# Both score maps of a token block in one three-bank PSUM tile, and a second bank for transposed probabilities

## The chip, the cores and the metric

The kernel runs on one core of one Trainium2 chip. The metric is the device time of one execution in microseconds (us). The engines are named as the profile names them: PE (TensorE, matmuls), DVE (VectorE), ACT (ScalarE), POOL (GpSimd) and SP (SyncE, which here issues the DMAs). PE writes its results to PSUM, which has eight banks of 2 KB in each partition (512 fp32 columns); DVE and ACT read them there.

## The reference

Two layers of a diffusion trunk. Each has a token-mixing part (a convolution branch and a differential-attention branch, merged by gates) and an MLP. There are 512 latent tokens and 256 context tokens; latent queries see all 768 keys, context queries the 256 context keys. In the second layer only the latent tokens have queries. What the change touches is the attention of one head:

```python
def block(qi):
    s = jnp.einsum('bqhcd,bkhcd->bhcqk', qi, keys,
                   preferred_element_type=jnp.float32) * scale
    p = jax.nn.softmax(s, axis=-1)
    w = p[:, :, 0] - lam * p[:, :, 1]
    return jnp.einsum('bhqk,bkhv->bqhv', w.astype(vals.dtype), vals)
```

Each of the 8 heads has two score maps (c = 0, 1), each with a softmax of its own; the weights are their difference.

## The kernel before, in words

Nearly all the work is matmuls in which fp32 operands are split into a high and a low part, so that one product takes three passes (`mm3`, lines 148 to 150: `qk` is the projection of queries and keys of the next head, `v` that of the values, both 256 columns a pass).

Attention runs head by head (`attend`, from line 960). A head has token blocks of 128 queries: four latent ones (t = 0 to 3, 768 keys) and, in the first layer, two context ones (t = 4, 5, 256 keys). For each block, `scores(t)` does for each of the two maps m: two passes over the keys on PE into a PSUM tile `S` (lines 988 and 990, in pieces of at most 512 columns), the row maximum on DVE (line 992), the exponential on ACT (line 995), which also sums the row. DVE then makes the weights of the difference in place (lines 999, 1000 and 1005: `e`). `turn(t)` transposes the weights on PE, three 128-key tiles at a time, into a PSUM tile `wT` (line 1018); ACT copies it into the high part `wth` and DVE subtracts for the low part `wtl` (lines 76 and 80, `split`). `values(u)` multiplies two blocks' transposed weights with the values into a PSUM tile `av`; `finish(u)` reduces its squares (`osq`, line 1044).

PSUM during attention: two banks for projections (pool `psA`), and what the pools `pS` and `pX` take. `pS` has two buffers for `S`; a map of 768 fp32 columns fills one and a half banks, and its tile takes two. `pX` has one bank with tag `tp` for `wT` and one with tag `av`. That is all eight.

The source runs a head's `scores`, `turn`, `values` and `finish` merged with filling work (projections of the next head, `qk` and `v`; for the last head the convolution's projections), by costs written in the yields. A scheduler then orders all instructions for each engine by a timing model of its own and the buffers that are free, and each engine works through its list in that order. A PSUM tile's buffer is given on when all that reads it is done. Between instructions of different engines on the same bank the framework puts a wait.

Of the kernel before, what the change touches and what calls it, by code (L numbers as in the profile page):

```python
# [8 lines left out]
F32 = mybir.dt.float32  # L9
# [5 lines left out]
P = 128  # L15
# [36 lines left out]
def trunk_kernel(  # L52
# [22 lines left out]
    def split(hi, lo, src, lo_eng=None):  # L75
        nc.scalar.activation(out=hi, in_=src, func=AF.Copy)  # L76
        with ExitStack() as later:
            if state["lows"]:
                later.enter_context(tc.issue_after(state["lows"]))
            return (lo_eng or nc.vector).tensor_tensor(out=lo, in0=src, in1=f32(hi), op=ALU.subtract)  # L80
# [65 lines left out]
    def mm3(ps, st, mv, first, last):  # L146
        (sh, sl), (mh, ml) = st, mv
        nc.tensor.matmul(ps, sh, mh, start=first, stop=False)  # L148
        nc.tensor.matmul(ps, sh, ml, start=False, stop=False)  # L149
        nc.tensor.matmul(ps, sl, mh, start=False, stop=last)  # L150
# [540 lines left out]
    for i in range(DEPTH):  # L691
# [13 lines left out]
        ap = apool.__enter__()  # L705
        state["tp"], state["nraw"] = ap, 1
        def tp_tile(name):
            return pX.tile([P, 512], F32, tag="tp", name=name)

        def hst(k, t):  # L710
            s = slice(t * P, t * P + P)
# [247 lines left out]
        def attend(h):  # L959

            QH, QL = QKt[h]
            vh, vl = Vt[h]
            U = {}

            def scores(t):
                u, j = t // 2, t % 2
                lat = u < 2
                nk, kb = (NTT, 0) if lat else (2, 4)
                nkey = nk * P
                if j == 0:  # L970
                    ng = 2 if lat else 1
                    U[u] = dict(
                        nk=nk, kb=kb, gw=nk // ng,
                        wT=[[ap.tile([P, 3, 256], F32R, tag=tg, name=f"{tg}{i}_{h}_{u}_{g}",
                                     bufs=3) for tg in ("wth", "wtl")] for g in range(ng)],
                        es2=ap.tile([P, 2], F32, tag="es2", name=f"es2{i}_{h}_{u}"))
                nm = f"{i}_{h}_{t}"
                ts = slice(t * P, t * P + P)
                es = []
                st = ap.tile([P, 8], F32, tag="st", name=f"st{nm}", bufs=4)  # L980
                for m in range(2):
                    S = pS.tile([P, 768], F32, tag="S", name=f"S{nm}_{m}")
                    for lo, hi in ((0, 512), (512, 768)):
                        lo = max(lo, kb * P)
                        if hi <= lo:
                            continue
                        o = slice(lo - kb * P, hi - kb * P)
                        nc.tensor.matmul(S[:, o], QH[:, m, ts], QH[:, 2 + m, lo:hi],
                                         start=True, stop=False)
                        nc.tensor.matmul(S[:, o], QL[:, m, ts], QH[:, 2 + m, lo:hi],  # L990
                                         start=False, stop=True)
                    nc.vector.tensor_reduce(out=st[:, m : m + 1], in_=S[:, :nkey], axis=AX.X,  # L992
                                            op=ALU.max, negate=True)
                    e = ap.tile([P, 768], F32, tag=f"e{m}", name=f"e{m}{nm}", bufs=2 - m)
                    nc.scalar.activation(out=e[:, :nkey], in_=S[:, :nkey], func=AF.Exp,  # L995
                                         bias=st[:, m : m + 1],
                                         accum_out=st[:, 2 + m : 3 + m])
                    es.append(e)
                nc.vector.reciprocal(st[:, 4:5], st[:, 3:4])
                nc.vector.tensor_scalar(st[:, 5:6], st[:, 4:5], st[:, 2:3], L["nlam"],  # L1000
                                        ALU.mult, ALU.mult)
                nc.gpsimd.tensor_tensor(out=st[:, 6:7], in0=st[:, 2:3], in1=st[:, 2:3],
                                        op=ALU.mult)
                nc.gpsimd.tensor_scalar(U[u]["es2"][:, j : j + 1], st[:, 6:7], EPS, None, ALU.mult)
                nc.vector.scalar_tensor_tensor(
                    out=es[0][:, :nkey], in0=es[1][:, :nkey], scalar=st[:, 5:6],
                    in1=es[0][:, :nkey], op0=ALU.mult, op1=ALU.add)
                W[t] = es[0]

            def turn(t):  # L1010
                u, j = t // 2, t % 2
                wt, gw = W.pop(t), U[u]["gw"]
                js = slice(j * P, j * P + P)
                for g, (th, tl) in enumerate(U[u]["wT"]):
                    tp = tp_tile(f"wT{i}_{h}_{t}_{g}")
                    for q in range(gw):
                        kk = g * gw + q
                        nc.tensor.transpose(tp[:, q * P : q * P + P],
                                            wt[:, kk * P : kk * P + P], ident)
                    split(th[:, :gw, js], tl[:, :gw, js],  # L1020
                          tp[:, : gw * P].rearrange("p (q d) -> p q d", q=gw))

            def values(u):
                d = U[u]
                nk, kb, gw = d["nk"], d["kb"], d["gw"]
                av = pX.tile([P, 512], F32, tag="av", name=f"av{i}_{h}_{u}")
                for kk in range(nk):
                    th, tl = d["wT"][kk // gw]
                    q = kk % gw
                    mm3(av[:, :256], (vh[:, kb + kk, :], vl[:, kb + kk, :]),  # L1030
                        (th[:, q, :], tl[:, q, :]), kk == 0, kk == nk - 1)
                sq = ap.tile([P, 256], F32, tag="osq", name=f"osq{i}_{h}_{u}", bufs=1)
                nc.scalar.activation(out=sq, in_=av[:, :256], func=AF.Square)
                uo = ap.tile([P, 256], F32, tag="uo", name=f"uo{i}_{h}_{u}")
                ended[:] = [nc.scalar.activation(out=uo, in_=av[:, :256], func=AF.Copy,
                                                 scale=L["ag"]).ins]
                nc.sync.dma_start(at_d[i][h, :, 256 * u : 256 * u + 256], uo)
                d["sq"], d["av"] = sq, av

            def finish(u):  # L1040
                d = U.pop(u)
                pc = d["av"][:, 256:258]
                for j in range(2):
                    nc.tensor.matmul(pc[:, j : j + 1], d["sq"][:, j * P : j * P + P],
                                     ones[:, 0:1], start=True, stop=True)
                r = rsall[:, h * qt_n + 2 * u : h * qt_n + 2 * u + 2]
                for j in range(2):
                    nc.scalar.activation(out=r[:, j : j + 1], in_=pc[:, j : j + 1],
                                         func=AF.Identity, scale=1.0 / P,
                                         bias=d["es2"][:, j : j + 1])  # L1050
                nc.gpsimd.tensor_tensor(out=r, in0=r, in1=mhalf[:, :2], op=ALU.pow)

            alone = h == H - 1
            W = {}
            nt = qt_n
            todo = []
            for t in range(nt):
                scores(t)
                yield 2.7 if t < 4 else 3.0 if alone else 0.9
                todo.append((0.7 if t < 4 else 0.25, turn, t))  # L1060
                if t % 2:
                    todo += [((2.0 if t < 4 else 0.7) + 2.0 * alone, values, t // 2),
                             (0.45 + 1.0 * alone, finish, t // 2)]
                if t == 0:
                    continue
                for _ in range(2):
                    if len(todo) > 1:
                        c_, f_, a_ = todo.pop(0)
                        f_(a_)
                        yield c_  # L1070
            carry.extend(todo)
# [88 lines left out]
        pS = pspool.__enter__()  # L1160
        psx = tc.tile_pool(name=f"psX{i}", bufs=1, space=PSUM, reuse_waits="tile")
        pX = psx.__enter__()
# [269 lines left out]
        for s in range(2):  # L1432
# [7 lines left out]
            for m in range(4):  # L1440
# [9 lines left out]
                for g in groups:  # L1450
                    rr[g.start] = gp.tile([P, 512], F32, tag="ar", bufs=3,
                                          name=f"mr{i}_{mb}_{g.start}")[:, : g.stop - g.start]
# [662 lines left out]
```

## Time and profile before

| | |
|---|---|
| median of 3 runs | 2258.76 us (2257.69 to 2258.91) |
| profiled execution, its own time | 2262.12 us |
| its span, first to last instruction | 2260.3 us |
| PE busy | 2217.1 us |
| DVE, ACT, POOL busy | 1651.7, 1045.5, 629.6 us |
| mean granted TensorE clock | 0.998 |

The profiled execution took 3.4 us more than the median; 1.8 us of its time lie outside the span. A matmul's record lasts longer than the distance to the next one, since they are pipelined, so a short pause of PE can hide in its busy time.

### The profile page before, as it was taken

What the parts mean: (1) busy time and instruction counts of PE and PEld (TensorE: products, weight loads), DVE (VectorE), ACT (ScalarE), POOL (GpSimd) and SP (SyncE); (2) the same over time, 40 slices, a digit from 0 to 9 for tenths busy, and PEclk for the clock granted to TensorE, in tenths of its full rate; (3) what the DMA queues carried; (4) which work ended last, traced back from release to release, by engine and by line L of the source; (5) the groups of instructions that cost most, each with busy time, mean ns of one, the idle gap of its engine ahead of it and who ended that gap; (6) DMA issues with size and microseconds to landing.
All of it is one profiled execution on the core that took longest, in us unless ns stands there. A gap on an engine that the chain in (4) does not pass through costs nothing.

```text
span 2260.3 us, 35793 instructions
## 1 busy us (share of the span) xinstructions
PE 2217.1 (98%) x14114; PEld 1999.1 (88%) x14114; DVE 1651.7 (73%) x2739; ACT 1045.5 (46%) x2035; POOL 629.6 (28%) x773
## 2 busy tenths in 40 slices
PE   8999999999999999999999999999999999999999
PEld 6999999888888999999999898999977888888887
DVE  6777777499767778788777457777769966657673
ACT  5555656432233264333445345565543333654541
POOL 1866666140000021111111346555613400000000
PEclk9999999999999999999999999999999999999999
DMA  9111101125354612332344521102114323443151
GB/s 310 57 48 45 48 29 49 64 98 171 128 176 140 205 50 64 108 115 91 131 145 144 173 76 57 46 27 64 45 61 162 117 82 127 144 143 100 56 186 38
DMA packets 202264, 232.59 MB, mean 103 GB/s; under 512 B 8864, under 2 KB 162928, under 8 KB 201968
## 3 DMA queue, kind: packets, MB, share of 16 engines
q1 hardware_dynamic: 202096, 230.30, 31.6%
q8 instruction: 111, 1.82, 0.3%
q14 instruction: 57, 0.47, 0.1%
HBM read 212.93 MB, written 17.35 MB: 102 GB/s over the span
## 4 chain that ended last, share of the span: by engine, by line
PE 77%; DVE 10%; POOL 4%; DMA 3%; ACT 3%; issue 2%; SPq 0%; DVEq 0%; POOLq 0%; ACTq 0%
PE r L157 4%; PE f L149 4%; PE f L150 3%; PE f L148 3%; PE r L148 3%; PE r L150 3%; PE r L149 3%; PE gt L148 3%; PE gt L149 3%; PE gt L150 3%; PE qk L148 2%; DMA ar<-in_w_ada_dram 2%; PE qk L149 2%; PE qk L150 2%; PE r L160 2%
## 5 line engine op out<-in xcount | busy, mean ns | idle before, releaser
L148 PE MATMUL qk<-h_wqk,h1h 128*128 128x256 f32 x640 | 183.7, 289 | 0.8 <-ACT h1h L76 0.7
L149 PE MATMUL qk<-l_wqk,h1h 128*128 128x256 f32 x640 | 181.1, 285 | 0.0
L150 PE MATMUL qk<-h_wqk,h1l 128*128 128x256 f32 x640 | 177.5, 285 | 0.0
L992 DVE TENSOR_REDUCE st<-S 128x1 f32<-128x768 f32 (+1 forms) x160 | 134.6, 846 | 52.2 <-PE S L990 51.1
L995 ACT ACTIVATE e<-S,st 128x768 f32<-128x768 f32 (+1 forms) x160 | 130.7, 820 | 29.8 <-DVE st L992 27.2
L149 PE MATMUL f<-h2hl,h_w 128*128 128x512 f32 (+1 forms) x416 | 143.3, 346 | 0.4 <-POOL h2hl L80 0.4
L148 PE MATMUL f<-h2hh,h_w 128*128 128x512 f32 (+1 forms) x416 | 142.6, 346 | 0.5 <-ACT fr L544 0.5
L150 PE MATMUL f<-h2hh,l_w 128*128 128x512 f32 (+1 forms) x416 | 142.6, 344 | 0.0
L148 PE MATMUL gt<-h1h,h_wg 128*128 128x512 f32 (+1 forms) x384 | 138.7, 361 | 0.0
L149 PE MATMUL gt<-h1l,h_wg 128*128 128x512 f32 (+1 forms) x384 | 136.7, 356 | 0.0
L150 PE MATMUL gt<-h1h,l_wg 128*128 128x512 f32 (+1 forms) x384 | 136.5, 356 | 0.0
L148 PEld LDWEIGHTS qk<-h_wqk,h1h 128*128 128x128 f32 x640 | 123.0, 192 | 3.3 <-ACT h1h L76 0.9
L157 PE MATMUL r<-F,wlor 128*128 128x512 f32 (+1 forms) x384 | 124.2, 339 | 0.7 <-DVE wlor L1660 0.7
L157 PE MATMUL r<-F,whir 128*128 128x512 f32 (+1 forms) x384 | 123.6, 338 | 0.2 <-ACT F L1603 0.2
L149 PEld LDWEIGHTS qk<-l_wqk,h1h 128*128 128x128 f32 x640 | 123.0, 192 | 0.1
L330 DVE SCALAR_TENSOR_TENSOR adaac<-ar,cvec,adaac 128x512 f32<-128x512 f32 x105 | 93.3, 911 | 38.2 <-DMA ar<-in_w_ada_dram 37.3
L150 PEld LDWEIGHTS qk<-h_wqk,h1l 128*128 128x128 f32 x640 | 120.6, 192 | 0.3 <-POOL h1l L80 0.2
L1236 DVE SCALAR_TENSOR_TENSOR cacc<-z,cols,cacc 128x783 f32<-128x783 f32 x120 | 118.8, 1047 | 0.0
L148 PE MATMUL v<-h_wv,h1h 128*128 128x256 f32 x384 | 112.2, 292 | 5.3 <-ACT rwc L874 2.6
L150 PE MATMUL v<-h_wv,h1l 128*128 128x256 f32 x384 | 108.9, 283 | 0.0
L149 PE MATMUL v<-l_wv,h1h 128*128 128x256 f32 x384 | 108.8, 283 | 0.0
L816 POOL TENSOR_TENSOR rqk<-rqk,mhalf 128x4 f32<-128x4 f32 x80 | 85.3, 1069 | 76.6 <-DVE rqk L815 74.1
(407 smaller groups left out, 7393.1 us busy)
## 6 DMA issues: line engine op xcount, KB each, us to landing
r_w<-in_w_mlp_dram SPq DMA_DIRECT2D x34, 1024.0 KB, 5.3
ada<-in_w_ada_dram SPq DMA_DIRECT2D x24, 1024.0 KB, 5.5
ar<-in_w_ada_dram SPq DMA_DIRECT2D x96, 256.0 KB, 3.4
r_wg<-in_w_in_dram SPq DMA_DIRECT2D x16, 1024.0 KB, 5.3
r_wqk<-in_w_in_dram SPq DMA_DIRECT2D x30, 512.0 KB, 5.2
rf<-in_w_mlp_dram SPq DMA_DIRECT2D x26, 512.0 KB, 4.0
rr<-in_w_mlp_dram SPq DMA_DIRECT2D x24, 512.0 KB, 3.7
r_wao<-in_w_attn_out_dram SPq DMA_DIRECT2D x8, 1024.0 KB, 5.0
```

Of the source, the lines that this page charges most:

```text
L148: nc.tensor.matmul(ps, sh, mh, start=first, stop=False)
L149: nc.tensor.matmul(ps, sh, ml, start=False, stop=False)
L150: nc.tensor.matmul(ps, sl, mh, start=False, stop=last)
L157: nc.tensor.matmul(ps, w[j][:, k, m0 : m0 + P], a(k)[0][:, toks], start=k + j == 0, stop=False)
L160: nc.tensor.matmul(ps, w[0][:, k, m0 : m0 + P], a(k)[1][:, toks], start=False, stop=k == nk - 1)
L330: nc.vector.scalar_tensor_tensor(out=a, in0=r, scalar=cvec[:, k, q : q + 1], in1=a, op0=ALU.mult, op1=ALU.add)
L816: nc.gpsimd.tensor_tensor(out=r, in0=r, in1=mhalf[:, :4], op=ALU.pow)
L992: nc.vector.tensor_reduce(out=st[:, m : m + 1], in_=S[:, :nkey], axis=AX.X, op=ALU.max, negate=True)
L995: nc.scalar.activation(out=e[:, :nkey], in_=S[:, :nkey], func=AF.Exp, bias=st[:, m : m + 1], accum_out=st[:, 2 + m : 3 + m])
L1236: nc.vector.scalar_tensor_tensor(out=(run if t < TAPS - 1 else ca[cc])[:, :CV], in0=zt[cc][:, t : t + CV], scalar=wcol, in1=run[:, :CV], o ...
```

## The change

The two maps of a block share one tile of 1536 columns, three banks, of which there is one (`bufs=1`). Map 0 lies in columns 0 to 767, map 1 in 768 to 1535, so that the middle bank holds the last 256 columns of map 0 and the first 256 of map 1. Map 1's pieces of a latent block are cut at the bank's end: 256 columns, then 512. The bank that is left over makes `tp` a tag of two.

```diff
         def tp_tile(name):
-            return pX.tile([P, 512], F32, tag="tp", name=name)
+            return pX.tile([P, 512], F32, tag="tp", name=name, bufs=2)
...
                 for m in range(2):
-                    S = pS.tile([P, 768], F32, tag="S", name=f"S{nm}_{m}")
-                    for lo, hi in ((0, 512), (512, 768)):
+                    if m == 0:
+                        both_s = pS.tile([P, 1536], F32, tag="S", name=f"S{nm}", bufs=1)
+                    S = both_s[:, 768 * m : 768 * m + 768]
+                    for lo, hi in ((0, 256), (256, 768)) if m and lat else ((0, 512), (512, 768)):
```

All lines of `attend` behind it stand two further down. No instruction is added or removed on any engine; the scheduler's order changes throughout both attentions, on all engines, and is the same elsewhere but for the places where the attentions begin and end. In the rows below, names end in head, block, (before) map and a running number; "waits" names the engines whose semaphores the instruction waits for ("Activation" is ACT).

On PE, second layer, head 0, block 1: before, both maps stand one behind the other.

```order
L988 MATMUL S_0_1_0_14866<-qk_0_14395 128x512 [waits PE_49,Activation_49]
L990 MATMUL S_0_1_0_14866<-qk_0_14395 128x512
L988 MATMUL S_0_1_0_14866<-qk_0_14395 128x256
L990 MATMUL S_0_1_0_14866<-qk_0_14395 128x256
L988 MATMUL S_0_1_1_14874<-qk_0_14395 128x512 [waits PE_49,Activation_49]
L990 MATMUL S_0_1_1_14874<-qk_0_14395 128x512
L988 MATMUL S_0_1_1_14874<-qk_0_14395 128x256
L990 MATMUL S_0_1_1_14874<-qk_0_14395 128x256
```

On PE, the same place now:

```order
L990 MATMUL S_0_1_14817<-qk_0_14347 128x512 [waits Activation_49]
L992 MATMUL S_0_1_14817<-qk_0_14347 128x512
L990 MATMUL S_0_1_14817<-qk_0_14347 128x256
L992 MATMUL S_0_1_14817<-qk_0_14347 128x256
L1020 MATMUL wT_0_0_0_14876<-cst,e_0_0_14755 128x128 [waits DVE_49]
L1020 MATMUL wT_0_0_0_14876<-cst,e_0_0_14755 128x128 x2
L1020 MATMUL wT_0_0_1_14882<-cst,e_0_0_14755 128x128 x3
L848 MATMUL qkT_1_2_14961<-cst,dup_1_2_14800 128x128 [waits DVE_49,Activation_49,Pool_49]
L848 MATMUL qkT_1_2_14961<-cst,dup_1_2_14800 128x128 x3
L872 MATMUL kcT_1_14969<-cst,kc_1_14921 128x128 [waits Activation_49]
L872 MATMUL kcT_1_14969<-cst,kc_1_14921 128x128
L990 MATMUL S_0_1_14817<-qk_0_14347 128x256 [waits Activation_49]
```

Map 1 has moved behind eleven transpositions and waits for ACT once more: the exponential of map 0 of the same block. The two groups of `wT` now follow each other. By the built program's waits the first map of every block waits in the same way for the exponential of the second map of the block before it.

On PE, first layer, the end of head 3, before: behind the second map of block 4 stands a whole projection of 24 passes, of which the first four are shown.

```order
L1018 MATMUL wT_3_2_0_3297<-cst,e_3_2_3142 128x128 [waits PE_49]
L1018 MATMUL wT_3_2_0_3297<-cst,e_3_2_3142 128x128 x2
L988 MATMUL S_3_4_1_3373<-qk_3_2304 128x256 [waits Activation_49]
L990 MATMUL S_3_4_1_3373<-qk_3_2304 128x256
L148 MATMUL v_2_4_3484<-h_wv_2_2774,h1h_338 128x256 [waits DVE_49]
L149 MATMUL v_2_4_3484<-l_wv_2_2775,h1h_338 128x256
L150 MATMUL v_2_4_3484<-h_wv_2_2774,h1l_339 128x256
L148 MATMUL v_2_4_3484<-h_wv_2_2774,h1h_338 128x256
```

On PE, the same place now, from the transpositions behind block 3's second map on:

```order
L848 MATMUL qkT_5_1_3835<-cst,dup_5_1_3641 128x128 [waits DVE_49,Activation_49,Pool_49]
L848 MATMUL qkT_5_1_3835<-cst,dup_5_1_3641 128x128 x3
L990 MATMUL S_3_4_3345<-qk_3_2291 128x256 [waits Activation_49]
L992 MATMUL S_3_4_3345<-qk_3_2291 128x256
L990 MATMUL S_3_4_3345<-qk_3_2291 128x256 [waits Activation_49]
L992 MATMUL S_3_4_3345<-qk_3_2291 128x256
L1020 MATMUL wT_3_3_0_3329<-cst,e_3_3_3261 128x128 [waits DVE_49]
L1020 MATMUL wT_3_3_0_3329<-cst,e_3_3_3261 128x128 x2
L1020 MATMUL wT_3_3_1_3335<-cst,e_3_3_3261 128x128 x3
L148 MATMUL av_3_1_3361<-wth_3_1_0_3110,vh_1_1429 128x256 [waits Activation_49]
L990 MATMUL S_3_5_3426<-qk_3_2291 128x256 [waits Activation_49]
L992 MATMUL S_3_5_3426<-qk_3_2291 128x256
```

The projections have moved to earlier places. Ahead of block 4's first map stand four transpositions, ahead of its second map nothing, ahead of block 5's first map six transpositions and one pass of `av`; each map waits for the exponential of the one before it. Behind these rows come 17 passes of `av`, 2 transpositions of `wT_3_4`, the second map of block 5, 2 single-column passes and the first map of head 4.

On DVE, the same place now (the maxima are L994, the weights of the difference L1007):

```order
L1001 RECIPROCAL st_3_3_3254<-st_3_3_3254 128x1 [waits Activation_49]
L1002 TENSOR_SCALAR st_3_3_3254<-st_3_3_3254,nlam_139 128x1 [waits DVE_49]
L817 TENSOR_TENSOR rw_5_3_3797<-rw_5_3_3797,rqk_5_3558 128x256 [waits Pool_49]
L994 TENSOR_REDUCE st_3_4_3344<-S_3_4_3345 128x1 [waits PE_49]
L1007 SCALAR_TENSOR_TENSOR e_3_3_3261<-e_3_3_3268,st_3_3_3254,e_3_3_3261 128x768 [waits DVE_49]
L834 TENSOR_TENSOR dup_5_3_3803<-ra_5_3_3804,rb_5_3_3805 128x4x64 [waits Pool_49]
L994 TENSOR_REDUCE st_3_4_3344<-S_3_4_3345 128x1 [waits PE_49,Activation_49]
L80 TENSOR_TENSOR wtl_3_1_0_3111<-wT_3_3_0_3329,wth_3_1_0_3110 128x3x128 [waits Activation_49]
L1001 RECIPROCAL st_3_4_3344<-st_3_4_3344 128x1 [waits Activation_49]
L1002 TENSOR_SCALAR st_3_4_3344<-st_3_4_3344,nlam_139 128x1 [waits DVE_49]
L80 TENSOR_TENSOR wtl_3_1_1_3113<-wT_3_3_1_3335,wth_3_1_1_3112 128x3x128 [waits Activation_49]
L1007 SCALAR_TENSOR_TENSOR e_3_4_3349<-e_3_4_3354,st_3_4_3344,e_3_4_3349 128x256 [waits DVE_49]
```

Other DVE work now stands between one map's exponential and the next map's maximum. The maximum of block 5's first map follows these rows.

## Rows read from the trace of the kernel before

**Rows 1.** The page, parts 1: busy time, share, instructions.

```profile
span 2260.3 us, 35793 instructions
PE 2217.1 (98%) x14114; PEld 1999.1 (88%) x14114; DVE 1651.7 (73%) x2739; ACT 1045.5 (46%) x2035; POOL 629.6 (28%) x773
```

**Rows 2.** Both attentions: from:to, length, then PE, PEld, DVE, ACT, POOL busy, PEclk.

```profile
85.00:452.00 367.00, 359.72 (x2754) 343.67 (x2754) 266.09 (x531) 211.41 (x528) 213.53 (x323) 1.00 0.15 46
...
1378.00:1715.00 337.00, 325.53 (x2386) 304.54 (x2384) 252.77 (x433) 189.03 (x420) 173.08 (x264) 1.00 0.17 51
```

**Rows 3.** PE's waits, whole span: us in total, times, longest us.

```profile
PE av L149 <- DVE wtl L80: 3.8, 5, 1.3
...
PE S L988 <- ACT e L995: 2.6, 3, 1.8
PE wT L1018 <- DVE wtl L80: 2.6, 6, 0.9
...
PE av L148 <- ACT wth L76: 1.0, 2, 0.6
```

**Rows 4.** Timeline, start of layer 0's attention: start us, duration us, engine, line, operation.

```profile
89.87 0.28 PE L988 MATMUL S<-qk 128*128 128x256 f32 x1
...
89.99 0.28 PE L990 MATMUL S<-qk 128*128 128x256 f32 x1
90.07 0.96 DVE L992 TENSOR_REDUCE st<-S 128x1 f32<-128x768 f32 x1 [0.92 <-PE S L990]
...
91.06 0.90 ACT L995 ACTIVATE e<-S,st 128x768 f32<-128x768 f32 x1 [0.34 <-DVE st L992]
...
92.11 0.50 PE L988 MATMUL S<-qk 128*128 128x512 f32 x1 [1.84 <-ACT e L995]
...
92.44 0.40 PE L990 MATMUL S<-qk 128*128 128x512 f32 x1
...
92.68 0.28 PE L988 MATMUL S<-qk 128*128 128x256 f32 x1
```

**Rows 5.** Busy time and granted clock (PEclk) before and behind that pause.

```profile
85.00:92.00 7.00, 5.27 (x39) 4.54 (x38) 5.08 (x10) 3.63 (x8) 7.00 (x11) 1.00 0.56 152
92.00:100.00 8.00, 7.89 (x48) 7.62 (x49) 6.52 (x13) 3.79 (x9) 6.02 (x11) 0.79 0.00 1
```

**Rows 6.** Groups on DVE: count, busy us, mean ns, idle before us.

```profile
L992 DVE TENSOR_REDUCE st<-S 128x1 f32<-128x768 f32 x128 | 121.0, 952 | 37.4 <-PE S L990 36.5
L80 DVE TENSOR_TENSOR wtl<-wT,wth 128x384 fp32r<-128x384 f32 x128 | 71.0, 555 | 36.5 <-ACT wth L76 34.7
L1005 DVE SCALAR_TENSOR_TENSOR e<-e,st,e 128x768 f32<-128x768 f32 x64 | 70.5, 1101 | 1.6
...
L1000 DVE TENSOR_SCALAR st<-st,nlam 128x1 f32<-128x1 f32 x80 | 21.5, 269 | 2.5 <-ACT e L995 1.4
...
L992 DVE TENSOR_REDUCE st<-S 128x1 f32<-128x256 f32 x32 | 13.5, 422 | 14.8 <-PE S L990 14.6
...
L1005 DVE SCALAR_TENSOR_TENSOR e<-e,st,e 128x256 f32<-128x256 f32 x16 | 8.2, 510 | 0.4
```

**Rows 7.** Groups on ACT, same columns.

```profile
L995 ACT ACTIVATE e<-S,st 128x768 f32<-128x768 f32 x128 | 115.6, 907 | 27.0 <-DVE st L992 24.5 <-DVE e L1005 2.5
L76 ACT ACTIVATE wth<-wT 128x384 fp32r<-128x384 f32 x128 | 63.0, 493 | 64.5 <-PE wT L1018 63.3
L852 ACT ACTIVATE qk<-qkT 128x512 fp32r<-128x512 f32 x80 | 47.9, 600 | 21.4 <-PE qkT L848 20.9
L995 ACT ACTIVATION_READ_ACCUMULATOR e<-S,st 128x1 f32 x160 | 33.2, 208 | 0.0
L1035 ACT ACTIVATE uo<-av,ag 128x256 f32<-128x256 f32 x40 | 18.9, 472 | 0.0
...
L995 ACT ACTIVATE e<-S,st 128x256 f32<-128x256 f32 x32 | 15.1, 471 | 2.7 <-DVE st L992 2.7
```

**Rows 8.** The chain that ended last: a group of four transpositions on PE.

```profile
99.30 0.44 PE qkT L848 x4
```

## The prediction

> **What bounds the kernel now.** I read the page first: PE is busy for 2217 of 2260 us, and no other engine comes near it [rows 1]. So the time falls only where PE stops less, and rises by every pause that PE gets. Next I cut the trace by stretch. In the two attentions PE's records cover 359.7 of 367 and 325.5 of 337 us [rows 2]: all that a better order could win there is bounded by some 19 us, and somewhat more for short pauses that the long records hide. Then PE's list of waits, which says how much of this the change can reach. The waits that hang on the one bank for transposed weights are those of `wT` for `wtl` (2.6 us) and of `av` for `wtl` and `wth` (3.8 and 1.0): 7.4 us together. Those of `S` for an exponential are 2.6 us [rows 3].
>
> Last I looked at the timeline at one of these, since it shows the whole chain of a map without a queue in it [rows 4]. The last pass of a map is issued at 89.99, its maximum runs from 90.07, its exponential from 91.06 for 0.90, and the map that waits for that buffer starts at 92.11. A pass of 256 columns takes PE 0.12 us (89.87 to 89.99), one of 512 twice as much (92.44 to 92.68). So from the end of a map's issue (90.11) to the start of the next one that needs its exponential pass **2.0 us** for a latent map. For a context map maximum and exponential are 422 and 471 ns instead of 952 and 907 [rows 6, 7], which leaves **1.04 us**. That pause is long enough for the clock too: in the stretch with it PE was busy for 5.27 of 7 us, and in the next one the granted clock was 0.79, a part of it at the lower level, 1.2 GHz instead of 2.4 [rows 5].
>
> **The change part by part.** No instruction comes or goes, and the work per engine stays. Two things change: the second bank for `wT`, and what a score map waits for.
>
> *The second bank.* It can take away at most the 7.4 us above. The changed order puts the two groups of `wT` of a block side by side, so I take all of it: **-7.4**. If the groups then wait for DVE's weights instead, it is less; at the least nothing.
>
> *The wait for the exponential.* Before, two tiles were in turn: a map waited for the exponential of the map two before it. Now each of the 160 maps waits for the exponential of the map just before it, inside a block as well as from block to block; the rows of the changed order show the first kind at both places. What hides the 2.0 us is the work that PE has between two maps. I went through PE's changed list and added it up for the 158 neighbouring pairs, at 0.12 us a pass of 256 columns, twice that for 512, and 0.11 for a transposition (four in 0.44 [rows 8]). In 137 pairs it is more than 2.0 us (1.04 behind a context map). In 21 it is less, and the shortfalls sum to **19.9 us**: 16.4 in layer 0, 3.5 in layer 1. The same count on the order before, at a distance of two maps, finds one place, 1.8 us: the pause of [rows 4]. What is new is 18.1 us. The 21 places are the ends of heads 1, 3, 5 and 6 of layer 0, where the four short context maps follow each other and the projections have been used up earlier, head 6 of layer 1, and five single ones.
>
> This is a lower bound, for it takes every maximum and every exponential as served at once, and DVE and ACT work through lists of their own. So I worked the end of head 3 through by hand, with the three engines' changed lists and the rows' durations. Time 0 is the start of block 3's second map.
> - Its exponential ends at 2.65; block 4's first map starts at 2.8.
> - Its sum is read (0.21), then DVE does the scalar product (0.27) and the reciprocal (taken as long), one product of `rw` (taken as 0.51), and only then the maximum; the second map of block 4 starts at 5.0 instead of 4.1.
> - DVE now does the difference (1.10) and `dup` (0.5) ahead of the next maximum, and ACT does `wth` (0.49) ahead of the exponential: block 5's first map starts at 7.2.
> - Both groups of `wtl` (0.56 each) and the difference of block 4 (0.51) stand ahead of the next maximum, and 17 passes of `av` lie on PE: block 5's second map starts at 9.9.
> - ACT does two copies of `av` (taken as 0.47 each), one `wth` and two copies of `qkT` (0.60 each) ahead of the last exponential: head 4's first map starts at 13.3.
>
> PE's own work in this stretch is 5.3 us, so it stands for 8.0 us, where the lower bound says 3.8: a factor of 2.1 [rows 6, 7]. Head 5 has the same order, heads 1 and 6 a similar one. I take the factor for all 18.1 us: **+38**. That is a choice: single places will come nearer to 1, the 137 covered pairs lose something now and then, and I let these cancel.
>
> For the upper bound I counted, pair by pair, what ACT and DVE have to do between two exponentials and between two maxima, and set it against PE's work between the maps. Where this is longer, it could cost the difference. Taken in full, without the slack that a neighbouring pair gives back, the sum over all pairs is 76 us.
>
> *The clock.* After the ends of four heads PE will have been busy for less than half of some 13 us, which is worse than the stretch of [rows 5]. In the 8 us behind that pause the granted share missing was 0.21 of 8, 1.7 us. If half of that falls into time in which PE waits anyway, four such places cost **+3.4**; the ends are 0 and 6.8.
>
> *A rule to weigh.* [rows 4] show a pass that starts only when the exponential on that buffer has ended, and the changed order keeps this wait for every map. The Trainium skill, PSUM — Partial Sum Buffer, section on bank collisions, says that PE writing and another engine reading in one bank at once is an error, and that one has to guard by bank. By it the latent blocks' second map has to wait in the middle bank, whatever its columns; but the context maps of one block lie in different banks (columns 0 and 768 on) and would be free of each other. The changed order makes them wait all the same. By the rule alone the sum would lose the context pairs inside blocks, a few us; I go by the order.
>
> **The sum.** -7.4 + 38 + 3.4 = +34. Against the profiled execution's 2262.1 us that is 2296; less the 3.4 us by which it lay above the median, **2293 us**.
>
> **The rivals.**
> 1. *The chain costs only what the lower bound says.* For it: in the pairs with cover DVE and ACT were idle 36.5 and 24.5 us waiting for PE's scores and for the maxima [rows 6, 7], so a maximum is often served at once. Against it: the hand-worked end of head 3. Then +18.1 - 7.4, less what else of the 2.6 us is absorbed, +8 to +11: 2267 to 2270.
> 2. *Everything adds up:* the full tally of 76 with a clock term of 6.8, and nothing won by the second bank: +81 at most, 2340. For it: DVE is busy for 266 of 367 us in layer 0's attention [rows 2] and the order is strict. Against it: an overfull pair is mostly followed by one with slack.
> 3. *Faster:* the second bank wins more than the chain costs. Its place is the row of 137 covered pairs: PE gets its 7.4 us, and pauses at the ends of heads let POOL and DVE catch up, which takes most of the remaining pauses out of both attentions. The whole 19 us of [rows 2] would have to go, against at least 18.1 us new: 2257 at the very best. It decides only if the chain needs far less than the 2.0 us of [rows 4]; with 1.0 us the shortfall would be 6.7 us and the sides even.
> 4. *No change,* the new pauses and those that go cancel: it needs the lower bound and nearly all of the old pauses gone: 2259.
>
> **How the numbers follow.** A run of this kernel can tell about 0.2%, 4.5 us, from no change. The likeliest case, 2280 to 2310, gets 0.55; the lower bound's case, up to 2280, 0.2; the upper one, over 2310, 0.12; no change 0.08; faster 0.05. The range reaches into the lower bound's case and into the full tally: 2267 to 2327. So faster 0.05, same 0.08, slower 0.87.
>
> **What would show it.** In the profile after, PE's busy time stays near 2217 us, and the span grows by pauses of PE. Among PE's waits, `S` for the exponential should rise from 2.6 us to 25 or more, most of it in layer 0, and at the ends of heads 1, 3, 5 and 6 two or three pauses of 1 to 3 us should follow each other, with the granted clock below 1 behind some of them. The waits of `wT` for `wtl` should all but vanish. The stretches between and behind the two attentions should keep their lengths within a few us. I would be wrong if PE's wait for the exponential stays under 10 us: then the chain is shorter than the one pause that I measured it by. I would be wrong in size if pauses stand at the many pairs with 3 to 5 us of cover, for then ACT and DVE are late everywhere, not just at the ends of heads.

## The result, and the profile after

The changed kernel takes 2321.85 us (median of 4 runs, 2320.87 to 2324.48), the kernel before, run beside it, 2258.84 (2257.69 to 2261.03): a ratio of 1.0278, 95% interval 1.0264 to 1.0292. It is 63 us slower. The forecast was 34 us slower, 2293, with 2267 to 2327 as range. So the direction and the range held, and the size was off by nearly half.

The page's first part of the kernel after, which answers to [rows 1]:

```profile
span 2322.7 us, 35751 instructions
PE 2243.8 (97%) x14114; PEld 2013.1 (87%) x14114; DVE 1657.7 (71%) x2739; ACT 1050.4 (45%) x2035; POOL 619.6 (27%) x773
```

The work is the same (PE 14114 passes in both), and the span is 62.4 us longer. PE's busy time did not stay at 2217, as the prediction had it: it rose by 26.7 us with no pass more, and PE's idle time by the other 35.7. That is the first sign of the clock. The span and the mean granted clock, kernel before and kernel after:

```profile
core 0: 2260.3 us, clock 0.998
```

```profile
core 0: 2322.7 us, clock 0.987
```

The granted share that was missing is 0.002 x 2260.3 = 4.5 us before and 0.013 x 2322.7 = 30.2 us after: **25.7 us more**, good to some 2 us, as the clock has three places. It is a bound and not a price: what is missing while PE has to wait costs nothing. An estimate of the price, from the two traces: each pass that PE began at the lower clock, taken at its distance to the next one there against its usual one (256 columns 0.21 us instead of 0.12, 512 columns 0.43 instead of 0.23, a transposition 0.21 instead of 0.11), comes to 21 us after and 3 before, **some 18 us more**. By it the rest of the 62.4 us, some 44, are pauses.

Where along the program the time went is read from two landmarks of each layer: the first pass of `gt` (the gates, behind the attention) and `rsT`, which waits for the last block of the last head. The rows of the tiles `gt` and `rsT` on PE (count, least, median and longest duration in ns, first and last start in us; `rsT` stands once per layer), before:

```profile
L148 PE MATMUL gt<-h1h,h_wg x384: 277/389/777, 479.2 to 1800.9; 128*128 128x512 f32 x128, 128*128 128x256 f32 x64
L1081 PE MATMUL rsT<-cst,rsall x2: 270/271/272, 516.6 to 1736.1; 128*48 128x128 f32 x1, 128*32 128x128 f32 x1
```

After:

```profile
L148 PE MATMUL gt<-h1h,h_wg x384: 277/389/796, 514.8 to 1863.3; 128*128 128x512 f32 x128, 128*128 128x256 f32 x64
L1083 PE MATMUL rsT<-cst,rsall x2: 270/270/271, 561.8 to 1798.5; 128*48 128x128 f32 x1, 128*32 128x128 f32 x1
```

Up to layer 0's first gate pass 35.6 us are lost (479.2 to 514.8), just behind it another 9.6 (`rsT` 45.2 later), in layer 1 up to its `rsT` another 17.2, and nothing behind that.

PE's waits after, which answer to [rows 3] (us in total, times, longest):

```profile
PE S L990 <- ACT e L997: 20.8, 17, 2.1
PE wT L1020 <- DVE e L1007: 8.7, 5, 6.3
PE adaps L266 <- DMA ada<-in_w_ada_dram: 6.4, 2, 5.4
...
PE av L149 <- DVE wtl L80: 1.4, 2, 1.0
...
PE av L148 <- ACT wth L76: 0.8, 3, 0.3
```

`S` for the exponential rose from 2.6 to 20.8 us, which is less than the 25 or more that were forecast, and `wT` for `wtl` is gone, as forecast. Two waits of over 5 us are new and were not: `wT` for the weights, and `adaps` for a load. On DVE and ACT, which answer to [rows 6, 7], the idle time ahead of the latent maxima rose from 37.4 to 86.7 us and ahead of the exponentials from 27.0 to 113.5:

```profile
L994 DVE TENSOR_REDUCE st<-S 128x1 f32<-128x768 f32 x128 | 122.2, 954 | 86.7 <-PE S L992 86.0
```

```profile
L997 ACT ACTIVATE e<-S,st 128x768 f32<-128x768 f32 x128 | 115.5, 903 | 113.5 <-DVE st L994 113.5
```

PE, DVE and ACT now wait for each other as links of one chain, at unchanged durations of 954 and 903 ns.

PE at the end of head 3, the place that the prediction worked through by hand, in the timeline of the kernel after:

```profile
277.84 0.28 PE L990 MATMUL S<-qk 128*128 128x256 f32 x1
...
280.79 0.39 PE L990 MATMUL S<-qk 128*128 128x256 f32 x1 [1.63 <-ACT e L997]
...
282.71 0.58 PE L990 MATMUL S<-qk 128*128 128x256 f32 x1 [1.42 <-ACT e L997]
...
285.50 0.58 PE L990 MATMUL S<-qk 128*128 128x256 f32 x1
...
286.52 0.41 PE L148 MATMUL av<-wth,vh 128*128 128x256 f32 x1
286.74 0.41 PE L149 MATMUL av<-wtl,vh 128*128 128x256 f32 x1
...
289.04 0.28 PE L148 MATMUL av<-wth,vh 128*128 128x256 f32 x1
289.16 0.28 PE L149 MATMUL av<-wtl,vh 128*128 128x256 f32 x1
...
289.54 0.36 PE L990 MATMUL S<-qk 128*128 128x256 f32 x1
...
292.10 0.57 PE L990 MATMUL S<-qk 128*128 128x512 f32 x1 [1.10 <-ACT e L997]
```

The first row is block 3's second map; the other five rows of L990 are the next maps. Between them `av` shows the clock: two passes stand 0.22 us apart at 286.52 and 0.12 at 289.04, for the same work. The stretches around it (from:to, length, busy PE, PEld, DVE, ACT, POOL, granted clock), which answer to [rows 5]:

```profile
272.00:279.00 7.00, 7.00 (x58) 6.60 (x57) 4.04 (x9) 3.44 (x10) 6.03 (x11) 1.00 0.05 19
279.00:285.50 6.50, 3.41 (x13) 2.23 (x11) 5.18 (x12) 2.66 (x8) 5.43 (x9) 0.74 0.00 0
285.50:292.40 6.90, 5.42 (x28) 5.13 (x29) 3.68 (x10) 3.65 (x12) 0.40 (x2) 0.75 0.06 19
292.40:296.00 3.60, 3.60 (x18) 3.44 (x17) 2.37 (x6) 0.99 (x2) 0.73 (x1) 0.53 0.02 5
```

While PE paused in the first 6.5 us the clock fell to its lower level, 1.2 GHz, and it stayed there for part of the two stretches that follow, in most of which PE had work: 0.26 x 6.5 + 0.25 x 6.9 + 0.47 x 3.6 = 5.1 us of granted clock are missing at this one head end.

### The profile page after: what moved, and what is told of

The parts are those of the page before. It is cut to its first block, busy times and chain, and to the rows that moved or that the text cites. A ratio compares the mean times of both kernels' runs of the same rounds, so it can differ in the third digit from the quotient of the medians.

```text
span 2322.7 us, 35751 instructions
## 1 busy us (share of the span) xinstructions
PE 2243.8 (97%) x14114; PEld 2013.1 (87%) x14114; DVE 1657.7 (71%) x2739; ACT 1050.4 (45%) x2035; POOL 619.6 (27%) x773
## 4 chain that ended last, share of the span: by engine, by line
PE 74%; DVE 9%; POOL 6%; ACT 5%; DMA 4%; issue 3%; SPq 0%; DVEq 0%; ACTq 0%; POOLq 0%
PE r L157 4%; PE f L149 3%; PE f L150 3%; PE f L148 3%; PE r L148 3%; PE r L150 3%; PE r L149 3%; PE gt L148 3%; PE gt L149 3%; PE gt L150 3%; PE qk L148 3%; PE qk L149 2%; DMA ar<-in_w_ada_dram 2%; PE qk L150 2%; PE r L160 2%
## 5 line engine op out<-in xcount | busy, mean ns | idle before, releaser
L994 DVE TENSOR_REDUCE st<-S 128x1 f32<-128x768 f32 (+1 forms) x160 | 135.6, 848 | 100.2 <-PE S L992 98.8
L990 PE MATMUL S<-qk 128*128 128x512 f32 (+1 forms) x288 | 101.2, 361 | 21.3 <-ACT e L997 20.8
L330 DVE SCALAR_TENSOR_TENSOR adaac<-ar,cvec,adaac 128x512 f32<-128x512 f32 x105 | 94.8, 925 | 35.7 <-DMA ar<-in_w_ada_dram 35.2
```

Of the source, the lines that this page charges most:

```text
L330: nc.vector.scalar_tensor_tensor(out=a, in0=r, scalar=cvec[:, k, q : q + 1], in1=a, op0=ALU.mult, op1=ALU.add)
```

## The experiments

In what follows "depth" is how many score tiles there are. The theory to be tested: the change costs what depth 1 costs, in pauses and in the clock behind them. Its rivals: the shared middle bank and the cut of map 1; the order that the second `tp` bank brings; ACT and DVE late at all maps, not at the short context maps; and the late ends of the attentions as a loss of their own.

**Depth 1 without the three-bank tile (depth1_tp2), and without the second `tp` bank too (depth1_tp1).** Both start from the kernel before:

```diff
-                    S = pS.tile([P, 768], F32, tag="S", name=f"S{nm}_{m}")
+                    S = pS.tile([P, 768], F32, tag="S", name=f"S{nm}_{m}", bufs=1)
```

the first also has `bufs=2` for `tp`.

> Each map has its own two-bank tile as before, but there is only one of them; tp has two banks. One bank stays unused. The chain theory (what costs is that each map waits for the exponential of the map just before it): 2322 us, within 5, and PE's wait of S for the exponential near 20.8 us. The layout theory (the shared middle bank or the cut of map 1 at 256 columns costs, by extra waits): 2250 to 2270 us.

> As the kernel before, with one score tile in place of two and still one bank for tp. The chain theory: 2322 plus what the second tp bank gives back, at most 7.4 us by the prediction: 2322 to 2332 us. If the second tp bank is worth nothing, the same as with it; if its own reordering is what costs, 2250 to 2300 us.

Measured: 2323.34 us (ratio 1.0273, 1.0253 to 1.0294) and 2319.43 (1.0255, 1.0237 to 1.0274). The first has the changed kernel's landmarks within 0.6 us (`gt` from 515.4, `rsT` at 562.3 and 1798.9) and the same wait:

```profile
PE S L988 <- ACT e L995: 20.8, 17, 2.1
```

So the layout, the middle bank and the cut are out; depth 1 alone makes the whole loss. And at depth 1 the second `tp` bank gives nothing back: without it the time is 4 us less, not up to 7.4 more, though `wT` then does wait 3.6 us for `wtl`. PE's wait of `S` is 16.4 us there instead of 20.8: what is not held up at the one place seems to be held up at the other.

**Each layer alone (layer0_only, layer1_only).** The kernel before, with `bufs=1` for `S` and `bufs=2` for `tp` in one layer only.

> One score tile and two tp banks in layer 0 alone; layer 1 as before. By the landmarks of the changed kernel (rsT of layer 0 at 561.8 instead of 516.6 us) layer 0 and its late end carry 45 us of the 63: 2300 to 2308 us, with rsT of layer 0 at 560 to 563 us. If the loss in layer 1 needs the one in layer 0 (or the other way about), the two layers alone don't add up to 63 us.

> One score tile and two tp banks in layer 1 alone; layer 0 as before. By the landmarks, 17 us: 2272 to 2281 us, of which some 13 at the late end of the last head (6.4 us of waiting for the weights and 13.7 us at half clock). By the prediction's count of shortfalls (3.5 us in this layer, times 2.1, less its part of the second bank's gain) it would be 2258 to 2264 us.

Measured: 2305.15 us (1.0195, 1.0179 to 1.0211) and 2278.26 (1.0074, 1.0057 to 1.0090), against 2261.55 of the kernel before on that chip: +43.6 and +16.7, 60 together. The layers add up, within what these runs can tell. Layer 1 costs 16.7 us, where the prediction's count gave it 3.

**The context maps given a second tile (context_own_bank).** From depth1_tp2, whose eighth bank is free:

```diff
-                    S = pS.tile([P, 768], F32, tag="S", name=f"S{nm}_{m}", bufs=1)
+                    own = not lat and m == 0
+                    S = (pX.tile([P, 512], F32, tag="Sc", name=f"S{nm}_{m}") if own else
+                         pS.tile([P, 768], F32, tag="S", name=f"S{nm}_{m}", bufs=1))
```

> The kernel of one score tile and two tp banks, with the unused bank as a tile of its own for the first map of each context block; so the context maps alternate between two tiles, and latent maps still have one. If the waits among the short context maps at the ends of heads make most of layer 0's loss, the first gate pass, at 515 us now, comes at 485 to 498 us, and the whole takes 2290 to 2308 us; layer 1 is as before this edit. If ACT and DVE are late at the covered latent maps too, 2312 us or more.

Measured: 2285.19 us (1.0113, 1.0098 to 1.0128), 38 us less than depth1_tp2 (36 by the ratios); mean clock 0.995. The landmarks, and the wait:

```profile
L148 PE MATMUL gt<-h1h,h_wg x384: 277/389/774, 485.4 to 1822.0; 128*128 128x512 f32 x128, 128*128 128x256 f32 x64
L1083 PE MATMUL rsT<-cst,rsall x2: 270/270/271, 522.0 to 1757.2; 128*48 128x128 f32 x1, 128*32 128x128 f32 x1
```

```profile
PE S L990 <- ACT e L997: 8.9, 8, 1.8
```

The first gate pass is back from 515.4 to 485.4, in the expected window, and layer 0's late end is gone as well (`rsT` 36.6 us behind it, before 37.4, after 47.0). The time, 5 us under the expected 2290, has this second part in it. With two tiles for the context maps layer 0 loses 5 us, with one 45; the 64 latent maps of the layer have one tile in both. So it is the short context maps, not ACT and DVE being late everywhere. One caution: the scheduler also moves the first context map ahead of its head's latent ones, so waiting and order are not separated here. The Trainium skill, PSUM — Partial Sum Buffer, section on bank collisions, guards by bank; by it maps in different banks are free of each other. No run here shows that by itself: the waits fell from 20.8 to 8.9 us once the first context map had a bank of its own, but it had a tile of its own along with it, and in the changed kernel the two context maps of a block lie in different banks (columns 0 and 768 on) and wait for each other all the same. What the built order guards is the whole tile.

**Work for PE in the pauses (extra_passes).** From depth1_tp2, ahead of 11 score maps of layer 0 (`scored` holds the last pass of the map before); the extra passes change nothing in the output:

```diff
+                    if i == 0 and (h, t, m) in {...}:
+                        with tc.issue_after(scored[0]):
+                            idle = pX.tile([P, 512], F32, tag="idle", name=f"idle{nm}_{m}", bufs=1)
+                            for _ in range(5):
+                                nc.tensor.matmul(idle, QH[:, m, ts], QH[:, 2 + m, 0:512],
+                                                 start=True, stop=True)
```

> The kernel of one score tile and two tp banks with the unused bank (2323 us), and 55 extra passes of 512 columns into that bank, whose result nobody reads: five (1.17 us) ahead of each of 11 score maps at the ends of heads 1, 3, 5 and 6 of layer 0, where PE paused for 0.5 to 2.3 us; 12.9 us of PE work more. If the lower clock behind the pauses is a cost of its own, the stretches at half clock in layer 0's attention shrink from some 31 us to under 10, and the time falls by 5 to 12 us in spite of the extra work: 2311 to 2318 us. If the slow stretches lie in time in which PE would wait anyway, as the prediction half assumed, 2322 to 2335 us.

Measured: 2329.53 us (1.0311, 1.0296 to 1.0326): 6 us slower than depth1_tp2 (9 by the ratios). The expected fall did not come, and the time lies where it was put if the slow stretches fall into time in which PE would wait anyway. The trace shows both sides of it. The end of head 3 in it and, below, in the changed kernel (depth1_tp2 has 43 passes and a clock of 0.75 there):

```profile
279.00:292.40 13.40, 12.47 (x85) 10.93 (x85) 9.44 (x22) 5.48 (x18) 4.27 (x9) 1.00 0.03 11
```

```profile
279.00:292.40 13.40, 8.83 (x41) 7.36 (x40) 8.86 (x21) 6.31 (x19) 5.83 (x11) 0.74 0.03 10
```

With the pauses filled the clock stays at 1.00 and PE does 85 passes in these 13.4 us, 15 of them extra, not 41. Over the whole run the mean clock is 0.990 instead of 0.985: 23.3 us missing instead of 34.8. But the first gate pass comes at 514.0 instead of 515.4. So 12.9 us of passes for nothing cost nothing up to there: they lie in pauses, and the clock that they kept up left little over. The chain has not become shorter: from block 3's second map to head 4's first one it is 14.2 us (275.80 to 290.03), in depth1_tp2 14.3 (278.24 to 292.55), and over the whole run `S` still waits 16.0 us for the exponential. The order changed as well, and with it part of the 85 passes: 17 of `qk` now stand ahead of head 4's first map, where depth1_tp2 has none, so the clock by itself is not separated here. The profiled execution (2327.3 us) is the fastest of the four; the few us that the others lie above it I can't place.

**The late ends (taps_held).** In the changed kernel the first tap of each run of the convolution on DVE is queued behind the last `wtl`:

```diff
-                        nc.vector.tensor_scalar(run[:, :CV], zt[cc][:, 0:CV], wcol,
...
+                        with tc.issue_after(lowest[0]):
+                            nc.vector.tensor_scalar(run[:, :CV], zt[cc][:, 0:CV], wcol,
...
```

(`lowest` holds the last low half that `turn` made.) What it is about is seen on PE at the end of layer 1 in the kernel after:

```profile
1764.96 0.39 PE L992 MATMUL S<-qk 128*128 128x512 f32 x1
1771.62 1.51 PE L1020 MATMUL wT<-cst,e 128*128 128x128 f32 x6 [6.27 <-DVE e L1007]
...
1774.63 0.58 PE L149 MATMUL av<-wtl,vh 128*128 128x256 f32 x1 [0.98 <-DVE wtl L80]
```

and on DVE at the same time, where `crun` are the taps:

```profile
1767.47 0.16 DVE L1001 RECIPROCAL st<-st 128x1 f32<-128x1 f32 x1 [1.06 <-ACT e L997]
1767.55 1.51 DVE L1234 TENSOR_SCALAR crun<-z,cols 128x512 f32<-128x512 f32 x2
1768.96 0.27 DVE L1002 TENSOR_SCALAR st<-st,nlam 128x1 f32<-128x1 f32 x1
1769.15 1.41 DVE L1238 SCALAR_TENSOR_TENSOR crun<-z,cols,crun 128x512 f32<-128x512 f32 x2
1770.46 1.01 DVE L1007 SCALAR_TENSOR_TENSOR e<-e,st,e 128x768 f32<-128x768 f32 x1
```

PE stands for 6.3 us behind its very last map: a chain of 2.1 us, 2.9 us of taps that DVE takes ahead, and the weights. The stretch behind that has half a clock:

```profile
1770.00:1784.00 14.00, 10.51 (x37) 8.84 (x38) 14.00 (x22) 4.11 (x8) 0.73 (x1) 0.51 0.25 73
```

0.49 x 14 = 6.9 us of granted clock are missing; not all of it is lost time, for PE is busy for 10.5 of these 14 us and DVE for all of them. In layer 0 the tail is longer: taps stand ahead of the last `wtl` there too, `uo` is late, SP has that store in its list ahead of the next load, and PE waits for that load:

```profile
531.88 0.41 DVE L80 TENSOR_TENSOR wtl<-wT,wth 128x256 fp32r<-128x256 f32 x1
...
533.58 0.47 ACT L1037 ACTIVATE uo<-av,ag 128x256 f32<-128x256 f32 x1
534.08 0.34 SPq L1039 DMA_DIRECT2D at_d<-uo  x1
...
534.58 1.02 SPq L107 DMA_DIRECT2D ada<-in_w_ada_dram  x2
...
540.12 1.51 PE L266 MATMUL adaps<-ada,cvec 128*32 128x256 f32 x12 [5.41 <-DMA ada<-in_w_ada_dram]
```

> The changed kernel, with the convolution's taps on DVE queued behind the last low half of the transposed weights of the last head, in both layers. If the late ends of the attentions come from the taps that DVE takes first, the wait of wT for the weights at the end of layer 1 (6.3 us), the 13.7 us at half clock behind it, the wait for the late ada load in layer 0 (5.4 us) and its 10.2 us at half clock go for the most part: 15 to 22 us less, 2300 to 2307 us. If the weights are late anyway and the taps only fill the time: 2317 to 2325 us.

Measured: 2314.52 us (1.0244, 1.0228 to 1.0259), 7 us less, which lies between the two times expected. The landmark and the waits:

```profile
L1083 PE MATMUL rsT<-cst,rsall x2: 270/270/271, 552.4 to 1785.3; 128*48 128x128 f32 x1, 128*32 128x128 f32 x1
```

```profile
PE wT L1020 <- DVE e L1007: 5.8, 4, 3.8
...
PE ya L149 <- DVE h1l L80: 4.1, 3, 2.5
...
PE ya L148 <- DVE cacc L1239: 1.9, 1, 1.9
```

At layer 0's `rsT` 9.4 us are won, all of its late end, with no wait of `adaps` left there. At layer 1's it is 13.2, but that is a running total: of the 9.4 only 5.8 are left at the first score pass of layer 1 (1416.7 instead of 1422.5), so layer 1 itself wins 7.4. And the span ends only 8.4 us earlier. In both layers the taps are now late, and `ya` waits for what stands behind them. The order on DVE makes the ends late, and mending it by delaying the taps moves a part of the wait on.

**The second bank without depth 1 (tp2_av_in_psA, tp2_shared_av, tp2_shared_pc_apart).** From the kernel before, with `bufs=2` for `tp`; in the first and in the second kernel `av` lives elsewhere:

```diff
-                av = pX.tile([P, 512], F32, tag="av", name=f"av{i}_{h}_{u}")
+                av = mm_tile(f"av{i}_{h}_{u}")
...
+                av = tp_tile(f"av{i}_{h}_{u}")
```

The third is the second with `pc` of `finish` in a `mm_tile` of its own.

> The second tp bank alone: the score tiles as before (two of two banks), two banks for tp, and av takes its bank from the two that the projections use. The waits of wT for wtl should go; by the prediction's term -7.4 us, so 2251 to 2259 us, unless av holds up the projections: then over 2262 us. The theory that the second bank (and the order that it brings) is what made the change slow: 2290 us or more.

> The second tp bank in another way: score tiles as before, and wT and av share the two banks that each had one of. A gain of the second bank of up to 7.4 us (2251 to 2259 us) if av holds its bank for short; no gain or a loss of a few us (2259 to 2266 us) where av keeps one of the two through its squares and wT is back to one. The theory that a second bank makes it slow: 2290 us or more.

> Two score tiles, wT and av sharing two banks (2252 us), and the row sums of av's squares in a bank of the projections in place of av's own bank, so that av's bank comes free some 1 to 2 us earlier. If the 4.3 us that wT waits there for the squares' sums is the rest that a bank can give: 2246 to 2250 us. If the projections lack the bank instead, as with av among them (2286 us): 2253 to 2270 us.

Measured: 2286.45 us (1.0111, 1.0094 to 1.0128), **2251.68 us (0.9955, 0.9938 to 0.9972)** and 2264.17 (1.0018, 1.0009 to 1.0028). I ran the one that beats both kernels once more:

> Again the kernel of two score tiles in which wT and av share two banks, with more rounds: 0.35 to 0.55% under the kernel before (2249 to 2253 us). If the first result was the chance of one chip: within 0.2% of before.

Measured: 2251.33 us (0.9956, 0.9943 to 0.9968). So a second bank for `wT` can win when it costs no score tile: about 10 us, nearly all in layer 1 (`rsT` at 514.8 and 1724.5 in the second run, 516.6 and 1736.1 before). `av` has two banks in turn there as well, so which of the two wins is not separated. `av` in the banks of the projections loses 25 us, close to what the theory of a slow second bank would have; the shared banks speak against that theory. There `v` waits, though these 7.4 us are not all of the 25:

```profile
PE v L148 <- DVE vl L80: 7.4, 10, 1.1
```

The last one was to save the 4.3 us in which `wT` waits for the squares' sums. It is 12 us slower than without, as expected if the projections lack the bank; but `v` waits for `vl` only 0.5 us there, so the cause is not shown.

## Why the prediction was right, and where its size failed

**The mechanism was right.** A map that waits for the exponential just before it pauses PE (depth1_tp2), most of all at the ends of heads 1, 3, 5 and 6 of layer 0: 13 of the 20.8 us of `S` stand there. The hand-worked end of head 3 put the next five maps at 2.8, 5.0, 7.2, 9.9 and 13.3 us; the timeline has 2.95, 4.87, 7.66, 11.70 and 14.26. PE lost 14.26 - 5.3 = 9.0 us there where 8.0 were forecast. That the sum fits so well is in part luck: the fourth link took 4.0 us instead of 2.7, with `av` at the lower clock, and the fifth 2.6 instead of 3.4. For layer 0's attention as a whole the prediction's terms give 14.6 us of new shortfall (16.4 less 1.8) x 2.1 + 3.4 for the clock, 34 us before the second bank's part; the first gate pass came 35.6 us later. Here too the total fits better than its parts. The stretch from the start of the attention to the first gate pass, before and after:

```profile
85.00:479.40 394.40, 385.85 (x2918) 367.17 (x2918) 291.38 (x563) 220.35 (x549) 221.96 (x330) 1.00 0.15 46
```

```profile
85.00:515.00 430.00, 402.12 (x2913) 376.40 (x2912) 283.44 (x548) 225.01 (x549) 214.53 (x330) 0.96 0.14 42
```

PE's busy time rose by 16.3 us and its idle time by 19.3. By the estimate above some 10 us are clock, forecast at 3.4, and some 26 pauses, forecast at 30.7: two errors that nearly cancel. The rivals of the bare lower bound, of no change and of a gain fell here. By its number the result lies in the case that I gave 0.12 (over 2310), but not by that case's mechanism: the covered latent pairs did not add up, context_own_bank gives layer 0 nearly all of its time back with them at depth 1 (in another order).

**Two mis-sized terms and one that was left out** make the missing 29 us: the ends 19, the second bank 7, the rest the chain and the clock.
- *The ends of the attentions*, forecast at nothing: "The stretches between and behind the two attentions should keep their lengths within a few us." The count went from map to map, and the last map of an attention has no next one, so nobody added up what stands behind it. It is 9.6 us behind layer 0 (gone in taps_held and in context_own_bank), and in layer 1 some 9.5 of the 17, of which taps_held won 7.4: counted by the columns that PE had taken in, the kernel after lies 44.4 us behind where the one before stands at 1378 us, 52.9 at 1710 and 62.4 at 1736. So 8.5 us went along layer 1's attention, where the count gave 3.5 x 2.1 = 7.4 before the bank's part. A last head that runs late finds the filling work used up, DVE and SP busy with other things first.
- *The clock*, +3.4, measured at some 18 us by the estimate, and at 25.7 us of missing granted share at the most. The step that failed was to take the loss behind one lone pause (1.7 us, [rows 5]) and halve it. The ends of heads have several pauses in a row, and 5.1 us are missing at the end of head 3 alone; behind layer 1's attention it is 6.9 and behind layer 0's, by the stretch 533 to 545 us with a granted clock of 0.57, 5.2. How little a missing share can cost is seen in depth1_tp2: it misses 34.8 us where the changed kernel misses 30.2, and its span is 0.4 us longer.
- *The second bank*, -7.4. The waits went for the most part (from 7.4 to 2.2 us), and the time did not: at depth 1 it is worth nothing (depth1_tp1 is 4 us faster without it). Waits read from a trace of depth 2 were booked as a gain in a kernel whose bound had changed.

**What remains open**: how much of context_own_bank's gain is the second tile and how much the earlier place of the context maps; where extra_passes lost its last few us; why the second bank wins in layer 1 more than the waits of [rows 3] hold; and how the loss splits between pauses and clock, beyond the estimate. I did not try to put the projections back behind the context maps by hand.

## What to carry to other kernels

Before taking a buffer from a chain that runs through several engines, count the work that the waiting engine has between two links, pair by pair, and most carefully where the links are short and the filling work ends; then go on counting behind the last link, to the first thing that needs its result. A wait that goes is a gain only while the same engine remains the bound. A freed bank may be had more cheaply: here two short-lived users sharing two banks gained 0.4% where taking a score tile for the same second bank lost 2.8%.

## What was not expected of the hardware

Pauses of 1.5 to 2 us, two or three in a row, brought TensorE's clock to 1.2 GHz for longer than they lasted: behind 3.1 us without work in 6.5 (279 to 285.5 us), `av`'s passes stood 0.22 us apart instead of 0.12 for some 3 us of continuous work, the clock rose for a moment, and after one more pause the next 3.6 us had a granted clock of 0.53. With passes that nobody needs in the pauses, and the order that came with them, it stayed at 1.00 (extra_passes). So some 44 us of pauses came with another 18 us of clock here, by the estimate above, and that second cost stands in the profile as busy time: 26.7 us more of it for the same 14114 passes, short pauses that the long records hide included.
